# Streaming the high and the low part of the activations through a weight tile in one 512-column matmul

## The chip, the core and the metric

The program runs on one core of a Trainium2 chip. Its time is device microseconds from start to end of one execution; smaller is better. TensorE (PE in the rows) multiplies: it loads a weight tile of 128 x 128 (PEld) and streams activation columns past it. VectorE (DVE) and ScalarE (ACT) do everything elementwise, SyncE (SP) issues the transfers from HBM.

## The reference

Two transformer-like blocks over 256 tokens of width 1024. The first has four layers (short convolution, a state-space mixer, an RWKV mixer, a short convolution again), each followed by a gate and a layer norm. The second has two layers of FFN, mixer and FFN, over 256 tokens and 256 context positions. Nearly all of the arithmetic is `x @ W` with fp32 weights that are used for one set of 256 columns, or for two:

```python
def short_conv_mixer(x, w_in, conv_k, w_out):
    bg, cg, h, z = jnp.split(x @ w_in, 4, axis=-1)
    ...
    return (bg * conv * jax.nn.silu(z)) @ w_out

def first_block(...):
    for i in range(DEPTH):
        ...
        r = DN_ALPHA * x + y
        r = r + (p[i] @ ple_proj[i]) * jax.nn.sigmoid(r @ ple_gate[i])
        x = layer_norm(r, ln_g[i], ln_b[i])

def swiglu(h, w1, w3, w2):
    return (jax.nn.silu(h @ w1) * (h @ w3)) @ w2

def half_ffn(h, g, shift, scale, gate, w1, w3, w2):
    return h + 0.5 * gate[:, None, :] * swiglu(modulate(rms_norm(h, g), shift, scale), w1, w3, w2)
```

The scales, shifts and gates of the second block are products of a small condition vector with large matrices (`ada_w`).

## The kernel before

Activations lie feature-major: 128 features on the partitions, 8 chunks of features, 256 positions along the free dimension (`S = 256`, `NCH = 8`). A weight is read from HBM in blocks of 128 output columns, all 8 input chunks side by side (512 KB). `get` (lines 588 to 604) issues the transfer and splits the block into two float32r tiles whose sum it is: ScalarE copies it into `whi` (line 599), VectorE subtracts to get `wlo` (line 600). Activations are split the same way by `split` (lines 606 to 608) into the two tiles that `pair` (lines 488, 489) gives: `hi` and `lo`, each of 8 chunks x 256 columns.

`mm3` (lines 610 to 624) multiplies: for each input chunk three matmuls of 256 columns, `whi` with the high part, `whi` with the low part, `wlo` with the high part, all added up in the same 256 columns of a PSUM bank of 512. Such a group of three is called a chunk in this text, and a column tile has 8 of them (6 in the last part of an FFN). Each matmul is an instruction of its own with its own weight load, so `whi` is loaded twice. All of them are issued at line 431 (`TensorE.matmul`).

`linear` (lines 659 to 669) runs over the column tiles of a weight and gives each PSUM result to a function `take`, which differs by caller: a copy, a Tanh, a multiplication that reads PSUM directly. `finish` (lines 750 to 762) adds the mixer's result to the residual; `ffn` (lines 1396 to 1434) computes 22 pairs of tiles (`ffn_in`, in three parts of 8, 8 and 6), each pair giving one chunk of `d`, and after each part 8 tiles of `ffn_out` that are added to the residual `x` or `ctx` with a gate. `add_gated` (lines 1441 to 1445) does that for the second block's mixers. `head_tile`, `values`, `low_rank`, `key` and `ple_proj` also multiply with 256 columns. `mm3t` (lines 636 to 645) is the token-major form, where the activations are the stationary side and the weights stream; for `ab_uv` it streams 512 columns at a time.

The order of instructions is chosen when the program is built. Generators of two streams (tokens, context) are woven by `weave`, and a planner's estimate of time (`now`) decides which goes on: float32r matmuls cost columns / 2400 us and 0.002 us (lines 425, 430), VectorE and ScalarE instructions 0.07 or 0.1 us and elements / 960 or / 1200. `ada` (lines 1340 to 1359) is side work of VectorE: for each of 144 tiles two reductions over 1024 columns (`junk`, line 1354), one tile every 6.5 to 12 planner-us (`GAPS`), unless VectorE is more than `SLACK` behind in the planner's view. PSUM pool `mm`, where all the products go, has 3 banks; split weights have 4 buffers, loaded ones 4, which `ada` shares.

## Time and profile before

| what | value |
|---|---|
| median of three runs | 2930.72 us (2926.54 to 2931.11) |
| span of the profiled execution, first to last instruction | 2931.2 us |
| PE busy | 2814.3 us, 23798 matmuls |
| weight loads busy | 2652.5 us, 23798 loads |
| VectorE busy | 2142.3 us |
| ScalarE busy | 1631.4 us |
| mean granted TensorE clock | 0.985 |

The page gives no time of the profiled execution besides its span. The span is 0.1 us above the highest of the three timed runs and 0.5 us (0.02%) above their median. Matmuls overlap in the records, and their ends are modelled: the rate of TensorE is read from the distance between two starts, not from the length of one.

### The profile page before, as it was taken

What the parts mean: (1) busy time and instruction counts of PE and PEld (TensorE: products, weight loads), DVE (VectorE), ACT (ScalarE), POOL (GpSimd) and SP (SyncE); (2) the same over time, 40 slices, a digit from 0 to 9 for tenths busy, and PEclk for the clock granted to TensorE, in tenths of its full rate; (3) what the DMA queues carried; (4) which work ended last, traced back from release to release, by engine and by line L of the source; (5) the groups of instructions that cost most, each with busy time, mean ns of one, the idle gap of its engine ahead of it and who ended that gap; (6) DMA issues with size and microseconds to landing.
All of it is one profiled execution on the core that took longest, in us unless ns stands there. A gap on an engine that the chain in (4) does not pass through costs nothing.

```text
span 2931.2 us, 58792 instructions
## 1 busy us (share of the span) xinstructions
PE 2814.3 (96%) x23798; PEld 2652.5 (90%) x23798; DVE 2142.3 (73%) x4116; ACT 1631.4 (56%) x3069; POOL 16.6 (1%) x42
## 2 busy tenths in 40 slices
PE   8989998899999999999999999999999999999999
PEld 8977788787999999998999978999999999996999
DVE  8876777666678788898898887877855336676655
ACT  5644556766646464778566766544522224466443
POOL 0000000000000000000000000000000000000000
PEclk9989998999999999999999999999999999999999
DMA  7632353200466666666675644666544323221554
GB/s 266 216 130 94 100 185 123 81 23 33 140 213 203 215 201 221 205 194 190 196 224 182 194 155 129 208 223 212 181 144 125 100 82 102 92 87 57 160 182 142
DMA packets 129296, 454.89 MB, mean 155 GB/s; under 512 B 14336, under 2 KB 18688, under 8 KB 128384
## 3 DMA queue, kind: packets, MB, share of 16 engines
q1 hardware_dynamic: 129024, 451.13, 48.3%
q8 instruction: 187, 3.06, 0.4%
q14 instruction: 85, 0.70, 0.1%
HBM read 450.02 MB, written 1.05 MB: 154 GB/s over the span
## 4 chain that ended last, share of the span: by engine, by line
PE 68%; DVE 14%; DMA 8%; ACT 6%; issue 4%; SPq 0%; DVEq 0%; ACTq 0%
PE ps_mm L431 56%; DMA w<-in_ada_dram 7%; PE ps_ca L431 5%; PE ps_cb L431 5%; DVE wlo L600 5%; DVE junk L1354 3%; ACT whi L599 2%; DVE tc L402 1%; PE ps_st L431 1%; PE ps_cb L435 1%; ACT L402 1%; ACT rw_b L402 1%; ACT tc L402 1%; DVE h_lo L402 1%; DMA w<-in_ffn_in_dram 1%
## 5 line engine op out<-in xcount | busy, mean ns | idle before, releaser
L599 ACT ACTIVATE whi<-w 128x1024 fp32r<-128x1024 f32 (+1 forms) x687 | 715.9, 1044 | 731.1 <-PE ps_mm L431 474.1
L600 DVE TENSOR_TENSOR wlo<-w,whi 128x1024 fp32r<-128x1024 f32 (+1 forms) x687 | 826.3, 1204 | 240.7 <-ACT whi L599 238.8
L431 PE MATMUL ps_mm<-h_hi,whi 128*128 128x256 f32 x3024 | 868.0, 289 | 6.1 <-ACT h_hi L402 4.4
L431 PE MATMUL ps_mm<-h_lo,whi 128*128 128x256 f32 x3024 | 856.0, 284 | 2.5 <-DVE h_lo L402 2.4
L431 PE MATMUL ps_mm<-h_hi,wlo 128*128 128x256 f32 x3024 | 853.2, 283 | 3.1 <-DVE wlo L600 3.0
L431 PEld LDWEIGHTS ps_mm<-h_hi,whi 128*128 128x128 f32 x3024 | 569.7, 189 | 15.8 <-ACT h_hi L402 6.3
L431 PEld LDWEIGHTS ps_mm<-h_lo,whi 128*128 128x128 f32 x3024 | 570.2, 189 | 8.7 <-DVE h_lo L402 3.7
L431 PEld LDWEIGHTS ps_mm<-h_hi,wlo 128*128 128x128 f32 x3024 | 570.9, 189 | 7.4 <-DVE wlo L600 4.9
L1354 DVE SCALAR_TENSOR_TENSOR junk<-w,cond 128x1024 bf16<-128x1024 f32 x288 | 351.9, 1222 | 125.9 <-DMA w<-in_ada_dram 124.8
L431 PE MATMUL ps_mm<-d_hi,whi 128*128 128x256 f32 x1232 | 353.4, 287 | 0.9 <-DVE ctx L402 0.4
L431 PE MATMUL ps_mm<-d_hi,wlo 128*128 128x256 f32 x1232 | 348.5, 283 | 3.6 <-DVE wlo L600 3.6
L431 PE MATMUL ps_mm<-d_lo,whi 128*128 128x256 f32 x1232 | 349.6, 284 | 0.0
L431 PEld LDWEIGHTS ps_mm<-d_hi,wlo 128*128 128x128 f32 x1232 | 233.2, 189 | 4.9 <-DVE wlo L600 4.7
L431 PEld LDWEIGHTS ps_mm<-d_hi,whi 128*128 128x128 f32 x1232 | 232.4, 189 | 4.0 <-issue 2.6
L431 PEld LDWEIGHTS ps_mm<-d_lo,whi 128*128 128x128 f32 x1232 | 232.4, 189 | 2.7 <-issue 1.6
L402 DVE TENSOR_TENSOR td<-td,ps_mm 128x256 f32<-128x256 f32 x154 | 64.5, 419 | 82.3 <-PE ps_mm L431 78.8
L402 ACT ACTIVATE d_hi<-td 128x256 fp32r<-128x256 f32 x154 | 63.0, 409 | 79.2 <-DVE td L402 78.4
L402 ACT ACT_TABLE_LOAD x81 | 103.9, 1283 | 2.5 <-PEq L1938 0.7
L431 PE MATMUL ps_mm<-x_hi,whi 128*128 128x256 f32 x256 | 73.6, 287 | 12.4 <-ACT whi L599 12.4
L402 ACT ACTIVATE tc<-tc 128x256 f32<-128x256 f32 x182 | 75.2, 413 | 6.0 <-DVE tc L402 3.1
L402 ACT ACTIVATE td<-ps_mm 128x256 f32<-128x256 f32 x154 | 57.1, 373 | 33.5 <-PE ps_mm L431 33.1
L431 PE MATMUL ps_mm<-xs_hi,whi 128*128 128x256 f32 x256 | 72.7, 284 | 2.7 <-ACT whi L599 1.6
(459 smaller groups left out, 5466.2 us busy)
## 6 DMA issues: line engine op xcount, KB each, us to landing
w<-in_ffn_in_dram SPq DMA_DIRECT2D x268, 512.0 KB, 4.0
w<-in_ada_dram SPq DMA_DIRECT2D x144, 512.0 KB, 4.3
w<-in_ffn_out_dram SPq DMA_DIRECT2D x96, 512.0 KB, 4.1
w<-in_conv_in_dram SPq DMA_DIRECT2D x64, 512.0 KB, 4.5
w<-in_ffn_out_dram SPq DMA_DIRECT2D x48, 384.0 KB, 3.5
w<-in_ab_in_dram SPq DMA_DIRECT2D x34, 512.0 KB, 4.4
w<-in_ple_gate_dram SPq DMA_DIRECT2D x32, 512.0 KB, 4.4
w<-in_conv_out_dram SPq DMA_DIRECT2D x16, 512.0 KB, 4.6
```

Source lines behind the costliest of these rows:

```text
L402: return f(**kw)
L431: self.t.matmul(out, lhsT=lhsT, rhs=rhs, start=start, stop=stop)
L435: self.t.transpose(out, in_, ident)
L599: nc.scalar.activation(out=hi[:, :n], in_=w[:, :n], func=AF.Copy)
L600: nc.vector.tensor_tensor(out=lo[:, :n], in0=w[:, :n], in1=hi[:, :n].bitcast(F32), op=ALU.subtract)
L1354: nc.vector.scalar_tensor_tensor(out=self.junk, in0=w, scalar=1.0, in1=cb[:, s], op0=ALU.mult, op1=ALU.mult, accum_out=m[:, t, s:s + 1])
```

## The change

`pair` lays the high and the low part of a chunk side by side (two tiles of 4 chunks, each chunk 2 x 256 columns); `Part` stands for one of the parts, and `both(k)` gives the 512 columns of chunk k. `mm3w` replaces the first two matmuls of a chunk by one of 512 columns that fills the whole bank; the third goes to its first half. The two halves of the bank then have to be summed. `total` does it with a ScalarE copy of the second half to SBUF and a VectorE addition, and its result takes the place of the PSUM operand in all of `linear`'s callers but three, and in `ffn_in`. In `finish`, `add_gated` and `ffn_out` (`halves`) a second VectorE addition takes the second half from PSUM. `head_tile`, `values`, `low_rank`, `key`, `ple_proj` and `mm3t` stay as they are. The planner's price of a float32r matmul under 512 columns rises by 0.01 us, and temporaries `te` get a third buffer. The rest of the diff takes out comments.

```diff
+class Part:
+    def __init__(self, tiles, q):
+        self.tiles, self.q = tiles, q
+    def __getitem__(self, at):
+        _, k, *t = at
+        n = NCH // 2
+        if isinstance(k, slice):
+            h = k.start // n
+            return self.tiles[h][:, k.start - h * n:k.stop - h * n, self.q]
+        return self.tiles[k // n][(slice(None), k % n, self.q, *t)]
+    def both(self, k):
+        return self.tiles[k // (NCH // 2)][:, k % (NCH // 2)].rearrange("p q t -> p (q t)")
...
         if rhs.dtype == F32R:
-            dur = n / 2400.0
+            dur = n / 2400.0 + (0.01 if n < 512 else 0.0)
...
     def pair(self, i, j, name):
-        return tuple(self.slot(k, [NCH, S], f"{name}_{q}", F32R) for k, q in ((i, "hi"), (j, "lo")))
+        t = [self.slot(k, [NCH // 2, 2, S], f"{name}_{q}", F32R) for k, q in ((i, "a"), (j, "b"))]
+        return Part(t, 0), Part(t, 1)
     def tmp(self, tag, n=S):
-        b = 2 if tag in ("td", "te") else 3
+        b = 2 if tag == "td" else 3
...
+    def mm3w(self, out, w, x, m=0, k0=0, start=True, stop=True):
+        T = self.T
+        (wh, wl), (xh, _) = w, x
+        kc = wh.shape[1]
+        for k in range(kc):
+            f = lambda t: t[:, k, m * 128:(m + 1) * 128]
+            T.matmul(out, lhsT=f(wh), rhs=xh.both(k0 + k), start=start and k == 0, stop=False)
+            T.matmul(out[:, :S], lhsT=f(wl), rhs=xh[:, k0 + k], start=False, stop=stop and k == kc - 1)
+    def total(self, ps, tag="te"):
+        t = self.tmp(tag)
+        self.A.activation(out=t, in_=ps[:, S:], func=AF.Copy)
+        self.V.tensor_tensor(out=t, in0=ps[:, :S], in1=t, op=ALU.add)
+        return t
     def mm3g(self, out, w, x, m=0):
+        mm = self.mm3w if out.shape[1] > S else self.mm3
...
-            self.mm3(out, part, x, m, k, k == 0, k + PIECE >= n)
+            mm(out, part, x, m, k, k == 0, k + PIECE >= n)
...
-    def linear(self, name, x, take, kc=8, mt=1, tiles=None):
+    def linear(self, name, x, take, kc=8, mt=1, tiles=None, halves=False):
...
-                yield from self.mm3g(ps[:, :S], w, x, m)
-                take(b * mt + m, ps[:, :S])
+                wide = isinstance(x, tuple) and isinstance(x[0], Part)
+                yield from self.mm3g(ps if wide else ps[:, :S], w, x, m)
+                if halves:
+                    take(b * mt + m, ps[:, :S], ps[:, S:])
+                else:
+                    take(b * mt + m, self.total(ps) if wide else ps[:, :S])
...
-        def take(m, ps):
+        def take(m, ps, more):
             self.V.scalar_tensor_tensor(out=r[:, m], in0=x[:, m], scalar=ALPHA, in1=ps, op0=ALU.mult, op1=ALU.add)
+            self.V.tensor_tensor(out=r[:, m], in0=r[:, m], in1=more, op=ALU.add)
...
-                yield from self.mm3g(ps[:, :S], w, xs)
-                t = self.tmp("td")
-                self.act(t, ps[:, :S], AF.Silu)
+                yield from self.mm3g(ps, w, xs)
+                t = self.total(ps, "td")
+                self.act(t, t, AF.Silu)
...
-                self.V.tensor_tensor(out=t, in0=t, in1=ps[:, :S], op=ALU.mult)
+                self.V.tensor_tensor(out=t, in0=t, in1=self.total(ps), op=ALU.mult)
...
-                    T.matmul(ps[:, :S], lhsT=wh[:, k], rhs=dh[:, q], start=k == 0, stop=False)
-                    T.matmul(ps[:, :S], lhsT=wh[:, k], rhs=dl[:, q], start=False, stop=False)
+                    T.matmul(ps, lhsT=wh[:, k], rhs=dh.both(q), start=k == 0, stop=False)
                     T.matmul(ps[:, :S], lhsT=wl[:, k], rhs=dh[:, q], start=False, stop=k == n - 1)
-                self.V.scalar_tensor_tensor(out=x[:, mt], in0=ps[:, :S], scalar=gt[:, mt:mt + 1], in1=x[:, mt], op0=ALU.mult, op1=ALU.add)
+                for o in (0, S):
+                    self.V.scalar_tensor_tensor(out=x[:, mt], in0=ps[:, o:o + S], scalar=gt[:, mt:mt + 1], in1=x[:, mt], op0=ALU.mult, op1=ALU.add)
...
-        def take(k, ps):
-            self.V.scalar_tensor_tensor(out=x[:, k], in0=ps, scalar=self.m(l, i, k, s), in1=x[:, k], op0=ALU.mult, op1=ALU.add)
+        def take(k, *pss):
+            for ps in pss:
+                self.V.scalar_tensor_tensor(out=x[:, k], in0=ps, scalar=self.m(l, i, k, s), in1=x[:, k], op0=ALU.mult, op1=ALU.add)
...
-        yield from self.linear("ab_out", os_, self.add_gated(l, 5, x, s))
+        yield from self.linear("ab_out", os_, self.add_gated(l, 5, x, s), halves=True)
...
-        yield from self.linear("cd_out", outs(), self.add_gated(l, 5, x, 0))
+        yield from self.linear("cd_out", outs(), self.add_gated(l, 5, x, 0), halves=True)
```

## Rows read from the trace of the kernel before

**Rows 1.** The page: busy us by engine (share, instructions); granted clock in 40 slices.

```profile
PE 2814.3 (96%) x23798; PEld 2652.5 (90%) x23798; DVE 2142.3 (73%) x4116; ACT 1631.4 (56%) x3069; POOL 16.6 (1%) x42
...
PEclk9989998999999999999999999999999999999999
```

**Rows 2.** Timeline of PE at 2000 us: start us, length us, instruction, out<-in, shapes.

```profile
2000.04 0.28 PE L431 MATMUL ps_mm<-h_hi,whi 128*128 128x256 f32 x1
2000.15 0.28 PE L431 MATMUL ps_mm<-h_lo,whi 128*128 128x256 f32 x1
...
2002.92 0.28 PE L431 MATMUL ps_mm<-h_hi,whi 128*128 128x256 f32 x1
```

**Rows 3.** Timeline of PE at 1235 us, the 512-column products of `ab_uv`.

```profile
1235.24 0.62 PE L431 MATMUL ps_mm<-whi,kvs 128*128 128x512 f32 x2
1235.70 0.39 PE L431 MATMUL ps_mm<-wlo,kvs 128*128 128x512 f32 x1
...
1236.64 0.39 PE L431 MATMUL ps_mm<-whi,kvs 128*128 128x512 f32 x1
1236.87 0.28 PE L431 MATMUL ps_cb<-kvs,whi 128*128 128x256 f32 x1
```

**Rows 4.** Timeline of the weight loads at 2000 us.

```profile
2000.28 0.19 PEld L431 LDWEIGHTS ps_mm<-h_hi,whi 128*128 128x128 f32 x1
2000.40 0.19 PEld L431 LDWEIGHTS ps_mm<-h_lo,whi 128*128 128x128 f32 x1
```

**Rows 5.** Timeline of PE at 1745 us, float32 products of the attention.

```profile
1745.49 1.02 PE L431 MATMUL ps_ca<-kava,qa 128*128 128x512 f32 x2
1746.35 1.02 PE L431 MATMUL ps_ca<-kb,qb 128*128 128x512 f32 x2
```

**Rows 6.** Groups of matmuls by operands: xcount | busy us, mean ns | idle before, releasers.

```profile
L431 PE MATMUL ps_mm<-h_hi,whi 128*128 128x256 f32 x3024 | 868.0, 289 | 6.1 <-ACT h_hi L402 4.4 <-ACT td L402 1.0 <-DVE td L402 0.6
...
L431 PE MATMUL ps_mm<-d_hi,whi 128*128 128x256 f32 x1232 | 353.4, 287 | 0.9 <-DVE ctx L402 0.4 <-ACT d_hi L402 0.4
...
L431 PE MATMUL ps_mm<-x_hi,whi 128*128 128x256 f32 x256 | 73.6, 287 | 12.4 <-ACT whi L599 12.4
...
L431 PE MATMUL ps_mm<-mix_hi,whi 128*128 128x256 f32 x208 | 60.1, 295 | 6.3 <-ACT mix_hi L402 4.3 <-ACT whi L599 1.8 <-ACT r L402 0.2
...
L431 PE MATMUL ps_mm<-o_hi,whi 128*128 128x256 f32 x192 | 54.8, 285 | 0.0
...
L431 PE MATMUL ps_mm<-gs_hi,whi 128*128 128x256 f32 x64 | 18.0, 281 | 0.0
```

**Rows 7.** Timeline of VectorE at 1479 us.

```profile
1478.81 1.23 DVE L600 TENSOR_TENSOR wlo<-w,whi 128x1024 fp32r<-128x1024 f32 x1
1479.94 0.43 DVE L402 TENSOR_TENSOR d_lo<-td,d_hi 128x256 fp32r<-128x256 f32 x1
1480.27 1.23 DVE L1354 SCALAR_TENSOR_TENSOR junk<-w,cond 128x1024 bf16<-128x1024 f32 x1
...
1492.34 0.48 DVE L402 SCALAR_TENSOR_TENSOR x<-ps_mm,gt,x 128x256 f32<-128x256 f32 x1
1492.73 0.95 DVE L600 TENSOR_TENSOR wlo<-w,whi 128x768 fp32r<-128x768 f32 x1
```

**Rows 8.** Groups of ScalarE instructions, the same columns: reading 256 columns of PSUM.

```profile
L402 ACT ACTIVATE td<-ps_mm 128x256 f32<-128x256 f32 x154 | 57.1, 373 | 33.5 <-PE ps_mm L431 33.1
```

**Rows 9.** Stretches: length; busy us (instructions) of PE, loads, DVE, ACT, POOL; clock; DMA.

```profile
879.00:1685.00 806.00, 783.63 (x6162) 757.05 (x6161) 691.42 (x1270) 532.14 (x913) 1.45 (x6) 1.00 0.63 202
...
2125.00:2418.00 293.00, 293.00 (x2444) 293.00 (x2443) 131.81 (x206) 78.07 (x121) 0.95 (x1) 1.00 0.36 112
...
1466.00:1539.00 73.00, 72.07 (x588) 71.19 (x587) 68.67 (x120) 49.77 (x84) 0.00 (x0) 1.00 0.72 225
```

**Rows 10.** Groups of matmuls between 879 and 1685 us, columns as in Rows 6.

```profile
L431 PE MATMUL ps_mm<-h_hi,whi 128*128 128x256 f32 x1051 | 303.7, 289 | 0.8 <-DVE td L402 0.6 <-ACT h_hi L402 0.2
...
L431 PE MATMUL ps_mm<-d_hi,whi 128*128 128x256 f32 x376 | 109.3, 291 | 0.9 <-DVE ctx L402 0.4 <-ACT d_hi L402 0.4
...
L431 PE MATMUL ps_mm<-xs_hi,whi 128*128 128x256 f32 x256 | 72.7, 284 | 2.7 <-ACT whi L599 1.6 <-DVE ta L402 1.2
```

**Rows 11.** Timeline of PE at the end of the first `ple_gate`.

```profile
168.66 0.28 PE L431 MATMUL ps_mm<-rs_hi,wlo 128*128 128x256 f32 x1
172.75 0.96 PE L431 MATMUL ps_st<-total,cs_base 128*128 128x256 f32 x2 [3.81 <-DVE total L402]
```

More of the change, by code (lines that the diff above doesn't have):

```diff
@@ L754, in finish @@
         rs = None if gate in RAW else self.pair(*slots, "rs")
-        def take(m, ps):
+        def take(m, ps, more):
             self.V.scalar_tensor_tensor(out=r[:, m], in0=x[:, m], scalar=ALPHA, in1=ps, op0=ALU.mult, op1=ALU.add)
+            self.V.tensor_tensor(out=r[:, m], in0=r[:, m], in1=more, op=ALU.add)
             if rs:
                 self.split(r[:, m], rs[0][:, m], rs[1][:, m])
-        yield from self.linear(w_out, g, take)
+        yield from self.linear(w_out, g, take, halves=True)
         return r, rs
@@ L1406, in ffn @@
                 ps = self.ps()
-                yield from self.mm3g(ps[:, :S], w, xs)
-                t = self.tmp("td")
-                self.act(t, ps[:, :S], AF.Silu)
+                yield from self.mm3g(ps, w, xs)
+                t = self.total(ps, "td")
+                self.act(t, t, AF.Silu)
                 w = yield (f"ffn_in{l}{h}", 2 * m + 1, 8, 128)
                 ps = self.ps()
-                yield from self.mm3g(ps[:, :S], w, xs)
-                self.V.tensor_tensor(out=t, in0=t, in1=ps[:, :S], op=ALU.mult)
+                yield from self.mm3g(ps, w, xs)
+                self.V.tensor_tensor(out=t, in0=t, in1=self.total(ps), op=ALU.mult)
                 self.split(t, dh[:, m % 8], dl[:, m % 8])
```

## The prediction

> **What bounds the kernel now.** I read the page's busy shares first: TensorE 96% of the span, VectorE 73%, ScalarE 56%, the clock at nine tenths or more in all but two of the forty slices [rows 1]. A busy PE need not be a full one, so the next view is the timeline of PE in a dense stretch: the reader is to look at the starts, not at the lengths. From 2000.04 to 2002.92 us there are 24 steps, 0.120 us each, with no idle time between them [rows 2]. A chunk of three matmuls thus takes 0.360 us. The weight loads start as often, 0.12 us apart, each 0.19 us long and beside the matmul before [rows 4]. Then the stretches: from 2125 to 2418 us PE is busy without a gap; from 879 to 1685 us it is idle for 22.4 of 806 us while VectorE is busy for 691 (86%); and in its fullest part, 1466 to 1539 us, VectorE is busy 94% and PE still 72.07 of 73 us [rows 9]. So TensorE's stream of columns sets the time nearly everywhere, and VectorE stands close behind it in 806 us of the span.
>
> **What the change takes from TensorE.** It touches the chunks that go through the wide path. By groups [rows 6]: h has 3024 chunks, of which 320 stay as they are (40 tiles of `head_tile` and `values`: 28 of `ab_in`, 8 of `cd_k`, 4 of `cd_q`, by 8); d 1232; x, xs and rs 256 each (x stands for three equal groups); mix 208 less 16 for `low_rank`; o and g 192 each; gs and ys 64 each. The sum is 2704 + 1232 + 768 + 192 + 384 + 128 = 5408 chunks.
>
> A chunk was three matmuls of 256 columns and becomes one of 512 and one of 256. The trace of before has a 512-column float32r matmul: `ab_uv` streams its weights that way. From 1235.24 to 1236.87 us there are 7 of them [rows 3], 0.233 us each, every one with a weight load of its own, as in the new form. So a chunk costs 0.233 + 0.120 = 0.353 us: 0.007 us less, and 5408 x 0.007 = 38 us. I take this value since it is the same operation with the same number of columns and loads; only the roles of weights and activations are swapped.
>
> The bounds: the worst is that the wide matmul costs what the two did, 0.240, and the gain is 0; a loss is excluded as long as rows 3 hold, which lie below that. The best comes from the nearest row with another type: the float32 products of 512 columns start 0.43 us apart (1745.49 to 1746.35 for two) [rows 5]. I take half of that, 0.215 us, as the far end, on the assumption (no row shows it) that float32 passes over its columns twice and float32r once; it is 25 ns under the pair, and the gain is 135 us.
>
> The rows show that a load lies beside the matmul before it, and that the removed load can be worth 7 ns at most. The Trainium skill, "TensorE: Matmul & The Clock Gate", Part 2, speaks against the change here: it says that loads are pulled ahead of running matmuls and read through a port of their own, so they take nothing from the stream. By that rule the gain is 0; rows 3 against rows 2 differ from it by the 7 ns. The same page's section on the back-to-back issue gap gives N / 2.4 + 2.5 ns, which is 216 ns for 512 columns; rows 3 show 233, so the trace doesn't agree, and by that figure with 0.120 for the narrow one the gain would be about 130 us.
>
> **What it adds.** `total` runs for the tiles that aren't halved: h 338, x, xs and rs 96, mix 24, ys 8, in all 466. Each costs ScalarE a copy of 256 columns from PSUM, 0.37 us by the group of such reads [rows 8], 172 us in all; and VectorE an addition, for which I take the distance from the start of `d_lo` to the next start, 0.33 us [rows 7]: 154 us. Where the result is halved, VectorE gets a second instruction: 32 additions (g and gs) of 0.33, and 192 gated ones (168 for d, 24 for o) of 0.39, from `x` to the next start [rows 7], 85 us together. VectorE gets 239 us, ScalarE 172.
>
> Where do they lie? ScalarE has 44% idle [rows 1], so its share is hidden; without that cover it would be those 172 us. VectorE's share is hidden where PE has no use for it: from 2125 to 2418 us it is busy for 132 of 293 us [rows 9]. From 879 to 1685 us it is not safe: there are 1051 - 224 chunks of h (28 narrow tiles off), 256 of xs and 376 of d [rows 10], which is 135 tiles at 0.33 and 51 at 0.39, 65 us. VectorE then has 756 us of work in 806 - 1459 x 0.007 = 796 us, 95%. What is queued behind an addition there is the next weight's `wlo`, for which the third matmul of a chunk waits, and a PSUM bank of three is given back one addition later. Since PE lost only 0.93 of 73 us at a VectorE of 94% [rows 9], I price this at about the stretch's idle time once more, 20 us; the bounds are 0 and the whole 65.
>
> At the end of a stage there is no cover: PE waits for the last tile's chain. After the first `ple_gate` it stood from 168.66 to 172.75 us [rows 11], and the chain gets a copy and an addition longer, 0.37 + 0.33 = 0.70 us. I count ten such ends without a second stream's work or with little of it: four gates, two ends of `conv_in`, `ssm_glu`, the three parts of the last FFN. That is 7 us. The rest is small: the wide matmul needs the low part one matmul sooner (0.12 us, at the same few ends), and the new layout and the third `te` buffer cost no time. The planner's price for a chunk goes from 3 x 0.1087 = 0.326 to 0.334, while the real one falls from 0.360 to 0.353; the side work, paced by the planner, comes 4% denser. It adds about 1% to VectorE's load and is in the 20 us. No transfer changes its size or number.
>
> The sum, against the profiled execution's 2931 us, 0.02% over the median: 2931 - 38 + 20 + 7 = 2920 us.
>
> **The rivals.**
> - *The wide matmul streams at full rate.* For it: float32's 0.43 us for 512 columns [rows 5]. Against it: rows 3, the same type and width. Time: 2931 - 135 + 7, and VectorE, which then has even less time beside it, for 30: 2833 us.
> - *VectorE becomes the bound between 879 and 1685 us, and the kernel gets slower.* The added 65 us then lengthen the stretch instead of filling its idle time, and the gain is what the other 3949 chunks give, 28 us: 2931 - 28 + 65 + 7 = 2975 us. It decides as soon as VectorE can't use more than the 86% it uses now, because of waits for `whi` and for PSUM; at 95% without a hold-up it doesn't. For it: the engines take turns on every tile, with few buffers between. Against it: the 94% of 1466 to 1539 us with a full PE.
> - *The removed load was hidden altogether.* The pair and the wide one cost the same, and only the additions remain: 2931 + 0 + 20 + 7 = 2958 us. Against it: rows 3, by 7 ns of 240, which is the whole gain and not much.
>
> **How the numbers follow.** The forecast has 0.52, with a range of its own from 2890 (savings of 8 ns, no contention) to 2950 (5 ns, contention of 40); full rate 0.16, VectorE as the bound 0.20, a hidden load 0.12. A measurement can tell about 0.2%, 5.9 us, from no change. Within the forecast 0.32 lies below 2925, 0.12 within 5.9 us of the time before, 0.08 above. So faster 0.32 + 0.16 = 0.48, same 0.12, slower 0.08 + 0.20 + 0.12 = 0.40. The range goes from 2840, just above the full rate, whose upper half it takes in, to 2980, just above VectorE as the bound.
>
> **What would show it.** The distance of starts in a dense stretch: 0.353 us a chunk confirms the main term, 0.335 the first rival, 0.360 the third. Between 2125 and 2418 us PE should stay gapless and do the same work in some 6 us less. Between 879 and 1685 us the stage's length and PE's idle time tell the second rival: some 45 us idle by the forecast, 85 or more if VectorE bounds it, with `wlo` and additions as what PE waits for. The count of matmuls must fall by 5408. The forecast is wrong if the wide matmul with activations streaming is not the 0.233 us of weights streaming, or if the order of instructions that the new prices give shifts a stage by more than these terms.

## The result and the profile after

The changed kernel takes 2954.61 us (median; 2951.0 to 2955.67), the kernel before 2930.91 beside it: ratio 1.0083, interval 1.0069 to 1.0097. It is slower by 24 us, where 2920 was forecast. The profiled execution spans 2952.3 us, 0.08% under the median. All differences between kernels below are differences of such ratios times 2931 us. The interval of one ratio reaches 3 to 7 us to either side, that of a difference between two of them 4 to 9, so a few us between two kernels say nothing.

The page of the changed kernel, as in [rows 1]:

```profile
PE 2787.4 (94%) x18390; PEld 2362.1 (80%) x18390; DVE 2384.1 (81%) x4811; ACT 1790.7 (61%) x3545; POOL 16.5 (1%) x42
...
PEclk9989998999999999999999999999999999999999
```

5408 matmuls are gone, as counted. VectorE has 241.8 us more (forecast 239), ScalarE 159.3 (forecast 172). So the counts and sizes of the added work were nearly right, and still the sum was not.

The timeline of PE in a full stretch, as in [rows 2] (start us, length us, instruction, out<-in, shapes, idle time before it and what ended it):

```profile
2012.70 0.39 PE L449 MATMUL ps_mm<-d_b,whi 128*128 128x512 f32 x1
2012.93 0.28 PE L449 MATMUL ps_mm<-d_b,wlo 128*128 128x256 f32 x1
2013.05 0.39 PE L449 MATMUL ps_mm<-d_b,whi 128*128 128x512 f32 x1
...
2013.98 0.28 PE L449 MATMUL ps_mm<-d_b,wlo 128*128 128x256 f32 x1
2014.10 0.39 PE L449 MATMUL ps_mm<-d_a,whi 128*128 128x512 f32 x1
2018.35 0.39 PE L449 MATMUL ps_mm<-d_a,wlo 128*128 128x256 f32 x1 [3.86 <-DVE wlo L619]
```

From 2012.70 to 2014.10 us there are four chunks: 0.350 us each, against 0.360 in [rows 2]. The wide matmul takes 0.232, the narrow one behind it 0.118 instead of 0.120. The last line is a stall of TensorE. The timeline of VectorE shows what it did in that time:

```profile
2014.00 1.23 DVE L1396 SCALAR_TENSOR_TENSOR junk<-w,cond 128x1024 bf16<-128x1024 f32 x1 [1.30 <-DMA w<-in_ada_dram]
2015.15 0.08 DVE L1396 DVE_READ_ACCUMULATOR junk<-w,cond 128x1 f32 x1
2015.15 0.48 DVE L420 SCALAR_TENSOR_TENSOR x<-ps_mm,gt,x 128x256 f32<-128x256 f32 x1
2015.55 1.21 DVE L1396 SCALAR_TENSOR_TENSOR junk<-w,cond 128x1024 bf16<-128x1024 f32 x1
2016.69 0.08 DVE L1396 DVE_READ_ACCUMULATOR junk<-w,cond 128x1 f32 x1
2016.69 0.48 DVE L420 SCALAR_TENSOR_TENSOR x<-ps_mm,gt,x 128x256 f32<-128x256 f32 x1
2017.09 1.21 DVE L619 TENSOR_TENSOR wlo<-w,whi 128x1024 fp32r<-128x1024 f32 x1
2018.22 0.47 DVE L420 SCALAR_TENSOR_TENSOR x<-ps_mm,gt,x 128x256 f32<-128x256 f32 x1
```

In these rows VectorE does one instruction after the other. The `wlo` that PE needs stands behind a reduction that waits 1.30 us for its own transfer, a second reduction, and two gated additions, one of which is new. Nothing here is long; it stands in one line.

This stall is not the work of the sums, though. In the run without them (`e1_no_sums`, below) the same product waits longer still, 4.68 us, behind a reduction that waits 3.40 us for its transfer; with the reductions shortened (`e6_light_side` and `e7_light_no_sums`) PE does not wait there at all. It is a stall of the side work. Its line without sums:

```profile
1975.20 0.39 PE L454 MATMUL ps_mm<-d_a,wlo 128*128 128x256 f32 x1 [4.68 <-DVE wlo L625]
```

A stall that the sums do lengthen is this one, the same product in both lines. In the changed kernel it waits for `ctx`, that is, for the addition that empties a bank; without sums it waits less, and for something else:

```profile
1160.93 0.76 PE L449 MATMUL ps_mm<-d_a,whi 128*128 128x512 f32 x1 [4.60 <-DVE ctx L420]
1149.97 0.77 PE L454 MATMUL ps_mm<-d_a,whi 128*128 128x512 f32 x1 [1.83 <-ACT h_b L425]
```

The stretches of [rows 9] (length; busy us of PE, loads, VectorE, ScalarE, GpSimd; granted clock; DMA), for the second one the place where the same stage now lies, and the time after that stall:

```profile
879.00:1685.00 806.00, 765.29 (x4407) 660.23 (x4407) 733.33 (x1433) 559.34 (x1035) 1.46 (x6) 0.98 0.60 194
...
2140.00:2435.00 295.00, 295.00 (x1688) 257.34 (x1687) 196.29 (x351) 109.47 (x204) 0.95 (x1) 1.00 0.42 134
...
2019.00:2020.00 1.00, 1.00 (x6) 0.86 (x5) 1.00 (x2) 0.00 (x0) 0.00 (x0) 0.59 0.70 287
2020.00:2022.00 2.00, 2.00 (x8) 1.71 (x8) 0.22 (x1) 0.00 (x0) 0.00 (x0) 0.50 0.92 272
2022.00:2024.00 2.00, 2.00 (x12) 1.72 (x12) 1.20 (x3) 1.06 (x1) 0.00 (x0) 0.85 0.62 252
```

PE is idle for 40.7 of 806 us in the first (22.4 before), and stays gapless in the second with 844 chunks in 295 us, 0.3495 each (before: 0.360). The first stretch has the same clock times as before but not quite the same work; the section on the prediction compares the stage. The last three lines: after 3.86 us of waiting PE works at full pace for a little under 1 us, and then without a gap but at a granted clock of 0.50, the lower level of 1.2 GHz, until about 2022.5 us. Its timeline there:

```profile
2019.97 0.63 PE L449 MATMUL ps_mm<-d_b,whi 128*128 128x512 f32 x1
2020.39 0.41 PE L449 MATMUL ps_mm<-d_b,wlo 128*128 128x256 f32 x1
2020.61 0.63 PE L449 MATMUL ps_mm<-d_b,whi 128*128 128x512 f32 x1
```

A chunk takes 0.64 us instead of 0.35. So this stall cost its 4 us and then five chunks at nearly twice their time, 1.4 us more. The Trainium skill, "TensorE: Matmul & The Clock Gate", HAM oscillation section, says that waits between bursts of matmuls drop the array back to half rate, and that this is paid at every such wait; at this stall the trace agrees, with 0.50 and 0.64 us. Not every wait here has such a tail: behind one of 2.32 us that ends at 1555.84 us the granted clock stays at 1.00.

What PE waited for, in total (us, times, longest), in the changed kernel:

```profile
PE ps_mm L449 <- DVE wlo L619: 23.7, 21, 3.9
PE ps_mm L449 <- ACT whi L618: 11.6, 4, 9.5
...
PE ps_mm L449 <- DVE ctx L420: 7.8, 4, 4.6
...
PE ps_st L449 <- DVE total L420: 6.6, 2, 3.8
...
PE ps_mm L449 <- DVE te L420: 4.6, 5, 2.2
PE ps_mm L449 <- DVE td L420: 3.8, 3, 2.6
...
PE ps_mm L449 <- DVE x L420: 2.6, 2, 1.8
```

`wlo` is a weight's low part, `whi` its high part. `ctx`, `te`, `td` and `x` are written by the instructions that empty a PSUM bank: a new tile's first product waits for one of the three banks.

### The profile page after: what moved, and what is told of

It reads as the page before. It is cut to its first block, busy times and chain, and to the rows that moved or that the text cites. A ratio compares the mean times of both kernels' runs of the same rounds, so it can differ in the third digit from the quotient of the medians.

```text
span 2952.3 us, 48981 instructions
## 1 busy us (share of the span) xinstructions
PE 2787.4 (94%) x18390; PEld 2362.1 (80%) x18390; DVE 2384.1 (81%) x4811; ACT 1790.7 (61%) x3545; POOL 16.5 (1%) x42
## 4 chain that ended last, share of the span: by engine, by line
PE 72%; DVE 13%; ACT 7%; DMA 6%; issue 2%; SPq 0%; ACTq 0%; DVEq 0%
PE ps_mm L449 59%; PE ps_ca L449 6%; PE ps_cb L449 4%; DVE wlo L619 4%; DMA w<-in_ada_dram 3%; DVE junk L1396 2%; ACT whi L618 2%; DVE tc L420 1%; PE ps_st L449 1%; PE ps_cb L453 1%; ACT L420 1%; ACT rw_b L420 1%; DMA w<-in_ab_in_dram 1%; ACT tc L420 1%; DVE r L420 1%
## 5 line engine op out<-in xcount | busy, mean ns | idle before, releaser
L449 PE MATMUL ps_mm<-h_a,whi 128*128 128x512 f32 (+1 forms) x1672 | 574.1, 387 | 16.1 <-DVE h_a L420 7.3
L449 PE MATMUL ps_mm<-h_b,whi 128*128 128x512 f32 (+1 forms) x1672 | 555.0, 376 | 2.1 <-DVE h_b L420 2.1
L449 PE MATMUL ps_mm<-h_a,wlo 128*128 128x256 f32 x1512 | 431.8, 286 | 10.7 <-DVE wlo L619 10.7
L449 PE MATMUL ps_mm<-h_b,wlo 128*128 128x256 f32 x1512 | 426.3, 283 | 0.0
L449 PEld LDWEIGHTS ps_mm<-h_a,whi 128*128 128x128 f32 x1672 | 307.3, 190 | 84.7 <-issue 11.5
L449 PEld LDWEIGHTS ps_mm<-h_b,whi 128*128 128x128 f32 x1672 | 304.3, 189 | 63.4 <-DVE h_b L420 3.5
L449 PEld LDWEIGHTS ps_mm<-h_a,wlo 128*128 128x128 f32 x1512 | 287.9, 190 | 20.0 <-DVE wlo L619 15.2
L449 PEld LDWEIGHTS ps_mm<-h_b,wlo 128*128 128x128 f32 x1512 | 285.2, 189 | 2.9 <-issue 1.4
L449 PE MATMUL ps_mm<-d_a,whi 128*128 128x512 f32 x672 | 251.9, 405 | 9.6 <-DVE ctx L420 7.1
L449 PE MATMUL ps_mm<-d_b,whi 128*128 128x512 f32 x560 | 207.4, 399 | 0.9 <-DVE d_b L420 0.9
L449 PEld LDWEIGHTS ps_mm<-d_a,whi 128*128 128x128 f32 x672 | 127.9, 190 | 42.8 <-issue 8.4
```

Of the source, the lines that this page charges most:

```text
L449: self.t.matmul(out, lhsT=lhsT, rhs=rhs, start=start, stop=stop)
```

## The experiments

Three things changed at once: the matmuls, the sums, and the order of all instructions, since the planner counts with other prices. The first four runs take them apart. To hold the order, an instruction can be counted by the planner without being issued (`ghost=True`), and a matmul can be counted with another number of columns.

### Wide or narrow, with or without sums, in one order

Without the sums (`e1_no_sums`):

```diff
-        self.A.activation(out=t, in_=ps[:, S:], func=AF.Copy)
-        self.V.tensor_tensor(out=t, in0=ps[:, :S], in1=t, op=ALU.add)
+        self.A.activation(out=t, in_=ps[:, S:], func=AF.Copy, ghost=True)
+        self.V.tensor_tensor(out=t, in0=ps[:, :S], in1=t, op=ALU.add, ghost=True)
+        self.alias[t.name] = ps[:, :S]     # users of t read the bank
...
-            self.V.tensor_tensor(out=r[:, m], in0=r[:, m], in1=more, op=ALU.add)
+            self.V.tensor_tensor(out=r[:, m], in0=r[:, m], in1=more, op=ALU.add, ghost=True)
```

and likewise for the second gated additions in `ffn_out` and `add_gated`.

> The changed kernel with its wide matmuls, but the instructions that sum the halves are not issued: no copy and no addition in `total`, no second addition in `finish`, `add_gated` and `ffn_out`; the users read the first half of the bank. The planner still counts them, so the order stays that of the changed kernel. Left out of the computation: the second half (high weight by low activations) is multiplied but not added. Theory S (the sums cost the time, in VectorE's and ScalarE's queues): 5408 chunks x 9.7 ns = 52 us under the kernel before, 2879 us, 75 us less than the changed kernel. Rival O (the order that the new prices give costs the time, not the sums): within 15 us of the changed kernel's 2955, so 2940 to 2960. In between, the two share it in that proportion.

Measured: 2897.87 us, ratio 0.9889 (0.9866 to 0.9912), 56.9 us under the changed kernel. That is a quarter less than theory S's 75 and far more than rival O's 15: the sums are most of the loss, not all of it.

Narrow matmuls with the sums (`e4_narrow_sums`), and narrow ones without sums (`e5_narrow_no_sums`):

```diff
-            T.matmul(out, lhsT=f(wh), rhs=xh.both(k0 + k), start=start and k == 0, stop=False)
+            if start and k == 0:
+                T.matmul(out, lhsT=f(wh), rhs=xh.both(k0 + k), start=True, stop=False)
+            else:
+                T.matmul(out[:, :S], lhsT=f(wh), rhs=xh[:, k0 + k], start=False, stop=False, cols=512)
+                T.matmul(out[:, S:], lhsT=f(wh), rhs=xl[:, k0 + k], start=False, stop=False, cols=0)
...
# e5: both into the first half, and the sums as ghosts
+            T.matmul(out[:, :S], lhsT=f(wh), rhs=xh[:, k0 + k], start=start and k == 0, stop=False, cols=512)
+            T.matmul(out[:, :S], lhsT=f(wh), rhs=xl[:, k0 + k], start=False, stop=False, cols=0)
```

and likewise in `ffn_out`.

> The changed kernel with its sums and its order, but the first two products of a chunk are two matmuls of 256 columns again, into the two halves of the bank (the first chunk of a tile stays wide). Seven eighths of the wide matmuls' gain are given up. Theory S with TensorE still the bound: the gain was 52 us, so 2955 + 45 = 3000 us. Rival V (VectorE is the bound in the stages with much side work, so TensorE's gain was mostly lost in waiting there): much less than 45 us is given up, 2965 to 2980 us. Rival O says nothing else than S here.

Measured: 2988.03 us, ratio 1.0203 (1.0179 to 1.0226), 35 us above the changed kernel. It lies between S (45) and V (10 to 25).

> Both taken back: three matmuls of 256 columns into one half as in the kernel before, no sums, but the order of instructions, the layout of the split activations and the third `te` buffer of the changed kernel (the planner still counts wide matmuls and sums). Theory S: order and layout cost nothing, 2931 us within 6. Rival O: the order is what costs, 2945 to 2985 us.

Measured: 2947.56 us, ratio 1.0055 (1.0035 to 1.0075): 16.1 us above the kernel before. Rival O holds here for its part: the same matmuls, the same elementwise work, another order, and 16 us. The layout of the split activations and the third `te` buffer came with it; no run separates them from the order. One difference can be counted: 692 splits of weights where the kernel before has 687. What that costs no run shows.

The three runs and the two kernels make a table of differences to the kernel before (us):

| | no sums | sums |
|---|---|---|
| narrow, order of before | 0 | |
| narrow, order of after | +16.1 | +59.5 (an eighth of it wide) |
| wide, order of after | -32.5 | +24.3 |

So the wide matmuls give 48.7 us where nothing else is added, 9.0 ns a chunk; the sums cost 56.9 us beside wide matmuls and some 49 beside narrow ones (43, and 6 for the eighth that is wide), where PE needs longer for a tile; and the order costs 16.1. 16.1 - 48.7 + 56.9 = 24.3 us, the whole result, since these are the steps from one kernel to the next; each is sure to 6 to 9 us.

That the order matters shows elsewhere too. The changed kernel with the planner's old price (`e2_old_price`):

```diff
-            dur = n / 2400.0 + (0.01 if n < 512 else 0.0)
+            dur = n / 2400.0
```

> The changed kernel with the planner's old price of a narrow float32r matmul (columns / 2400, without the added 0.01 us). The planner then believes a chunk to cost 0.324 us instead of 0.334. Theory S: nothing but noise of the order, 2955 us within 8. Rival O, in the form that the new price is at fault: 2935 us or less.

Measured: 2937.66 us, ratio 1.0026 (1.0016 to 1.0036), 16.7 us under the changed kernel. Theory S missed (within 8 us of 2955); rival O (2935 or less) missed by 3 us and is the nearer. This order is neither that of before nor that of the changed kernel, so it proves no figure for the latter. The new price by itself, in the kernel before (`e3_before_new_price`, the same line the other way round):

> The kernel before, with one edit: the planner's price of a float32r matmul under 512 columns is 0.01 us higher, as in the changed kernel. Nothing else changes but the order that the planner finds. If the new price makes the order worse by itself: 2940 us or more. If the 17 us of order that the changed kernel carries come with the price only beside the counted sums: 2931 us within 6.

Measured: 2969.51 us, ratio 1.0133 (1.0117 to 1.0150): 39 us slower from 0.01 us in a planner's table. And with the side work's pace stretched in proportion (`e17_price_pace`, `GAPS = (7.1, 10.9, 13.1, 13.1)`):

> The kernel before with the new price (2969 us), and the side work's intervals longer by 9% (`GAPS` 7.1, 10.9, 13.1, 13.1), as the planner's time for three matmuls is. If the 39 us came from side work that the higher price makes denser in real time: back to 2931 us within 10. If from the order in which the streams' instructions are woven: 2950 us or more.

Measured: 2977.25 us, ratio 1.0165 (1.0148 to 1.0182). The denser side work is not the reason; how the streams' instructions are woven is what is left. Four orders of the same narrow work lie 0 (`e11_same_order_narrow`, below), 16, 39 and 48 us above the kernel before, and I found no rule in them.

### What in the sums costs

The side work on VectorE shortened (`junk` over 64 columns instead of 1024), with and without sums:

```diff
-  nc.vector.scalar_tensor_tensor(out=self.junk, in0=w, scalar=1.0, in1=cb[:, s], ...)
+  nc.vector.scalar_tensor_tensor(out=self.junk[:, :64], in0=w[:, :64], scalar=1.0, in1=cb[:, s, :64], ...)
```

> The changed kernel, with the two reductions of each `ada` tile over 64 columns instead of 1024 (the transfer stays whole, the planner's price too). Left out of the computation: all but the first 64 columns of those products, so the modulation is another. VectorE loses about 288 x 1.0 us of work. To be compared with the next run, which is the same without the sums. Theory C (the additions cost by standing in VectorE's queue among the side work): the sums cost less than 20 us here instead of 57, so less than 20 us over the next run. Rival H (they cost by what they add to the chain of a tile, the copy, the addition and the later PSUM bank, whatever else VectorE does): 45 us or more over the next run.

> The same shortened reductions in the changed kernel without its sums (left out: the second half of each bank, and all but 64 columns of the `ada` products). Gives the base for the run before. By itself: between 2870 and 2898 us; the side work cost at most the 28 us of waits for `wlo` and for norms that are left without the sums.

Measured: ratios 0.9905 (0.9885 to 0.9924) and 0.9751 (0.9735 to 0.9767), 2899.75 and 2855.31 us. Without sums the side work had cost 40 us, more than I had set as the most. The sums cost 45 us here instead of 57. So side work in VectorE's queue makes the sums dearer by about 12 us, with an error of some 11; theory C, my own from the prediction, is at most a part of the matter. Rival H (45 or more) is just met.

Only the copies (`e8_copies_only`: the copy issued, the addition a ghost), and only the second additions of the halved results (`e13_halves_only`: the copies and additions of `total` as ghosts):

> The changed kernel with the copies of `total` on ScalarE (466 of 0.37 us) but without any of the 690 instructions that they add to VectorE; the users read the first half. Left out of the computation: the second half is not added. Order of the changed kernel. Theory C: near the run without copies and additions, 2898 to 2910 us. Rival A (ScalarE's queue is at fault: the copies delay `whi`): 2935 us or more.

> The changed kernel in its order, without the copies and additions of `total` (466 tiles), but with the second additions of `finish`, `add_gated` and `ffn_out` (224 instructions of VectorE, some 81 of its 239 us of added work). Left out of the computation: the second half of the banks that `total` sums. Theory Q: in proportion to VectorE's time, 2898 + 19 = 2917 us. Theory W: these additions wait for no other engine than before, 2898 to 2908 us.

Measured: ratios 0.9971 (0.9958 to 0.9984) and 0.9977 (0.9967 to 0.9987), 24 and 26 us above the run without sums. Both theories missed on the copies: 466 copies that nobody reads, on an engine that was idle 44% of the time, cost 24 us. In the prediction they cost nothing. They did not do it by delaying weights, as rival A has it: PE waits 16.0 us for `whi` and 9.7 for `wlo`, against 14.1 and 10.9 in the run without sums; what grew are waits for other results of ScalarE, `pp` from 0.5 to 6.0 and `td` from 2.4 to 5.5. On the additions theory W missed, and Q (19) came nearer: 224 instructions on VectorE cost some 0.12 us each, though each only follows one that had to wait anyway.

The same amount of work, on data that nothing waits for (`e10_loose_sums`):

```diff
+        nc.scalar.activation(out=t, in_=src, func=AF.Copy)                       # src: a constant
+        nc.vector.tensor_tensor(out=self.junk[:, :S], in0=src, in1=src, op=ALU.add)
```

> The changed kernel without its sums, as in the run without copies and additions (2898 us), but with the same number of copies (ScalarE) and additions (VectorE) of 128 x 256 elements on a constant tile: the same work, for which nothing waits and which waits for nothing, so it may slip to other places of its engine's queue. Left out of the computation: the second half of each bank. Theory Q (the time that the sums take of VectorE and ScalarE is what costs): near the changed kernel, 2940 to 2955 us. Theory W (their place costs: they wait for the tile's last matmul and for each other, with weight splits and other tiles' work behind them in the queues, and the tile's result comes later): 2898 to 2912 us.

Measured: 2906.62 us, ratio 0.9921 (0.9906 to 0.9935). Its page:

```profile
PE 2766.3 (95%) x18390; PEld 2350.0 (81%) x18390; DVE 2376.0 (82%) x4810; ACT 1788.3 (62%) x3550; POOL 16.5 (1%) x42
```

VectorE and ScalarE are as busy as in the changed kernel (2384.1 and 1790.7 us), with as many instructions, and the kernel is 47 us faster. The work as such costs 9 us, with an error of 8; the other 47 come from where it stands. This is theory W (2898 to 2912), and against theory Q: equal busy shares go with a difference of 47 us. Two limits of the run: the loose instructions read SBUF where the sums read PSUM, and not all of the copies are free of waits. Before the 154 into `td` ScalarE is idle for 89 us in all, until their buffer is free:

```profile
L667 ACT ACTIVATE td<-cs_base 128x256 f32<-128x256 f32 x154 | 63.6, 414 | 89.2 <-DVE d_a L425 50.9 <-DVE d_b L425 37.9
```

Two groups of the changed kernel (busy us, mean ns, then idle time of the engine just before them and what ended it) show the standing:

```profile
L420 ACT ACTIVATE te<-ps_mm 128x256 f32<-128x256 f32 x314 | 115.6, 370 | 51.5 <-PE ps_mm L449 51.0
```

```profile
L420 DVE TENSOR_TENSOR te<-ps_mm,te 128x256 f32<-128x256 f32 x312 | 129.8, 417 | 39.1 <-ACT te L420 37.9
```

ScalarE stands for 51 us at the head of its queue until PE has ended a tile, and VectorE for 38 us until ScalarE has copied it; what is queued behind waits too, and a late PE makes them both late. How much of the 57 us comes of that these rows don't tell: a wait at the head of ScalarE's queue is not dear by itself, as the 89 us of the loose copies show.

### Is it the weights behind, or the banks?

What can stand behind a sum is a weight's split; what stands before PE is a bank. First, the second additions put behind the next tile's weight split (`e14_delayed`):

```diff
+  late = m1 < 22 or last
+  if late and mt:
+      self.tc.keep_in_program_order(second())    # the tile before's second half
   for o in (0, S):
-      self.V.scalar_tensor_tensor(out=x[:, mt], in0=ps[:, o:o + S], ...)
+      self.V.scalar_tensor_tensor(out=x[:, mt], in0=ps[:, o:o + S], ..., ghost=late and o > 0)
+  second = lambda mt=mt, ps=ps: nc.vector.scalar_tensor_tensor(out=x[:, mt], in0=ps[:, S:], ...)
+  if late and mt == NCH - 1:
+      second()
```

The last tile of each of the 15 parts keeps its second addition in place, so 105 of the 120 move.

> The changed kernel, with one edit: in `ffn_out` (all parts after which no squares are taken, 120 of the 168 tiles) the second addition of a tile is issued after the next tile's weight split instead of right behind the first addition. Same work, same planner's order. Theory W1 (the sums cost because weight splits stand behind them in VectorE's queue): the second additions cost 25 us in all, 224 of them; for the 120 that move, up to 13 us come back: 2941 to 2950 us. Rival W2 (they cost because their own tile's bank and result are ready later): no gain or a loss, since these results come later still: 2953 us or more.

Measured: 2960.92 us, ratio 1.0109 (1.0093 to 1.0125), 7.6 us above the changed kernel. W2 holds; W1's gain did not come. The run also keeps the banks longer, so the time alone would not refute W1. PE's waits say more:

```profile
PE ps_mm L449 <- DVE wlo L619: 23.9, 23, 3.6
PE ps_mm L449 <- ACT whi L618: 11.5, 3, 9.7
PE ps_mm L449 <- DVE te L420: 9.1, 12, 2.2
```

Those for weight parts are as long as in the changed kernel (23.7 and 11.6), so taking the additions out of the way of the splits did not bring the splits sooner where PE waits for them; those for `te` doubled. Then four banks in one ring instead of three and one, with and without sums:

```diff
-        self.psum = {n: self.pool(es, "p_" + n, b, PSUM) for n, b in BANKS.items()}
+        self.psum = {n: self.pool(es, "p_" + n, b, PSUM) for n, b in dict(mm=4, ca=2, cb=2).items()}
+        self.psum["st"] = self.psum["mm"]
```

> The changed kernel, with the PSUM bank of the pool `st` (sums over partitions) put into the pool `mm`: four banks that products and those sums use in turn, instead of three and one. The planner still counts three and one, so the order stays. Theory B (a tile's sum gives its bank back later, and the first matmul of a coming tile waits for it): the sums' cost, which is this run less the next, falls from 57 us to 40 or less. Rival W1 (weight splits come late behind the sums): it stays above 50.

> The same four banks in the changed kernel without its sums (2898 us with three and one). Left out of the computation: the second half of each bank. By theory B banks are hardly waited for here, so 2885 to 2900 us; the products that end a norm (`st`) now wait in the same ring, which may cost some us.

Measured: ratios 1.0053 (1.0038 to 1.0068) and 0.9872 (0.9854 to 0.9889), 2943.48 and 2893.29 us. The fourth bank helps the changed kernel by 9 us; the 5 us of the one without sums are within the errors. The sums still cost 53 us, within the errors the 57 of before. Theory B (40 or less) falls as the one cause; that the cost stays above 50 is what rival W1 had forecast here. The waits of the changed kernel with four banks tell why:

```profile
PE ps_mm L449 <- DVE wlo L620: 27.8, 28, 4.0
PE ps_mm L449 <- ACT whi L619: 17.0, 7, 9.5
...
PE ps_mm L449 <- DVE te L420: 1.3, 3, 0.6
```

The waits for `te` fell from 4.6 to 1.3 us, and those for `ctx`, `td` and `x` are no longer among the thirty longest, but `wlo` rose from 23.7 to 27.8 and `whi` from 11.6 to 17.0. The stall had changed its name: with three banks the sums show at the banks, with four at the weights.

In the run without sums and with three banks the waits for weights, and the one for `total`, read:

```profile
PE ps_mm L454 <- ACT whi L624: 14.1, 4, 10.5
PE ps_mm L454 <- DVE wlo L625: 10.9, 11, 4.7
...
PE ps_st L454 <- DVE total L425: 3.6, 2, 2.8
```

Last, where does the 57 us stand in TensorE's time? I took every distance between two starts on PE in the run without sums and in the changed kernel, and put what exceeds the full-clock distance (0.232, 0.118 to 0.120 us) under what ended the idle time, or, where PE was not idle and the distance was about twice that, under the low clock:

| us over full pace | no sums | sums | more |
|---|---|---|---|
| idle until a result of VectorE or ScalarE is there, or a bank | 21.5 | 42.8 | 21.3 |
| idle until a weight part is there | 18.0 | 30.0 | 12.0 |
| idle before sums over partitions, attention and the like | 18.7 | 24.2 | 5.5 |
| not idle, at half the clock | 36.9 | 50.1 | 13.2 |
| not idle, other short delays | 30.3 | 34.7 | 4.4 |
| sum | 125.4 | 181.8 | 56.4 |

Nearly a quarter of what the sums cost is not waiting at all, but slow chunks, as after 2019 us above. Counted in the same way, the run with loose sums has some 27 us of idle time for weight parts, 22 for results or banks, and 35 at half the clock. So work in VectorE's and ScalarE's queues that no product needs already makes the splits of weights late, and this is about its 9 us; the longer waits for results and banks and the slow chunks come only with the sums in their place.

### A version that beats both

Set stage against stage, the run without sums and the changed kernel drift apart by 2 us up to the weights of the second `conv_in` (885 and 887 us), by 32 more until the second `ab_out` (1785 and 1819), by 20 more until `cd_f` (2391 and 2445), and by 4 after that. So the wide form was kept where the sums cost little: `conv_in0`, `conv_out0` and the FFNs (1,0) and (1,1), with the old price (`e9_wide_slack`):

```diff
+WIDE = ('conv_in0', 'conv_out0', 'ffn10', 'ffn11')
...
+                wide = isinstance(x, tuple) and isinstance(x[0], Part) and name in WIDE
```

> Wide matmuls and sums only where the comparison of the runs with and without sums shows small cost: `conv_in0`, `conv_out0`, and the FFNs (1,0) and (1,1); three narrow matmuls without sums elsewhere, with the planner's old price. Gain 9.2 ns x about 1850 chunks = 17 us, cost of the sums there about 3 us: 2931 - 14 = 2917 us if the order does no harm. Rival: by the order the time moves 10 us either way, 2907 to 2927; rival H: sums cost everywhere alike, 690 tiles for 57 us, here about 270 of them for 22 us: 2936 us.

Measured: 2913.35 us, ratio 0.9954 (0.9937 to 0.9971). And the same order with narrow matmuls everywhere and no sums (`e11_same_order_narrow`):

> The kernel with wide matmuls in four stages only (2913 us), in its order, with three narrow matmuls into one half and no sums everywhere. Its difference to that kernel is the net worth of the wide form in those stages. If the wide form earns what was worked out (17 us of matmuls less 3 of sums), 2927 us; if that kernel's lead over the kernel before is only a better order, 2918 us or less.

Measured: 2930.00 us, ratio 1.0000 (0.9989 to 1.0012). The 13.5 us (with an error of 6) are the wide form's own, not a luckier order's: 1904 chunks at 9.0 ns are 17 us, and the sums there cost 4.

Then the `ffn_out` stages of all other FFNs too, where a tile takes only one more instruction of VectorE and none of ScalarE, the planner's order untouched; without and with the delay of the second addition (the diff of the delay is the one above):

```diff
-                    if wide:
-                        T.matmul(ps, lhsT=wh[:, k], rhs=dh.both(q), start=k == 0, stop=False)
-                    else:
-                        T.matmul(ps[:, :S], lhsT=wh[:, k], rhs=dh[:, q], start=k == 0, stop=False)
-                        T.matmul(ps[:, :S], lhsT=wh[:, k], rhs=dl[:, q], start=False, stop=False)
+                    T.matmul(ps, lhsT=wh[:, k], rhs=dh.both(q), start=k == 0, stop=False, cols=None if wide else 516.8)
```

> The same without the delay: each second addition right behind the first. By the price of 25 us for 224 (0.11 us each): 2913 - 6.5 + 11 = 2918 us. If these stages have slack: 2907 us.

> The kernel with wide matmuls in four stages (2913 us), with its order, plus wide matmuls in the `ffn_out` stages of the other FFNs (704 chunks, 96 tiles with one more addition), the second addition issued after the next weight's split where no squares follow. The planner isn't told. Gain 704 x 9.2 ns = 6.5 us; cost, by the 25 us for 224 such additions, 11 us if they stood in front, less behind the split. W1: 2908 to 2914 us; W2: 2917 us or more.

Measured: 2904.51 us, ratio 0.9912 (0.9896 to 0.9928), and 2914.50 us, ratio 0.9952 (0.9938 to 0.9967). The first is the best of all complete versions, 26 us under the kernel before. Its page:

```profile
PE 2781.6 (96%) x21190; PEld 2501.1 (86%) x21190; DVE 2266.2 (78%) x4457; ACT 1687.6 (58%) x3235; POOL 16.5 (1%) x42
```

The delayed run lies between W1 (2914 at most) and W2 (2917 or more), but the delay costs 11.7 us, a second time against W1. The 12 us from the 704 chunks have an error of 7, so the 6.3 that 9.0 ns each give are within it.

## Why the prediction was wrong, step by step

- *The chunk's price.* The mechanism was right, the size low: 0.353 us forecast from [rows 2] and [rows 3], 0.350 measured; 38 us forecast, 48.7 measured by the two runs without sums. The gap is 2 to 3 ns a chunk, most of it the narrow matmul behind a wide one (0.118, not 0.120), and 5408 chunks make 11 us of it. The Trainium skill, "TensorE: Matmul & The Clock Gate", Part 2, says that loading the next weights takes no read bandwidth from the running matmul. By that a removed load would be worth 0, as the rival of the hidden load has it; a removed pair of load and matmul is worth 9 ns here, which part of the pair is open. The full-rate rival would have needed 0.215 us for 512 columns, and 0.232 was measured; that float32 passes over its columns twice, which its price assumed, no run shows.
- *The counts.* 5408 matmuls, 690 instructions on VectorE with 242 us, 159 us on ScalarE: right.
- *The copies at nothing.* This step failed. ScalarE's 44% of idle time was named as the cover for 172 us of copies. Alone they cost 24 us. Idle time of an engine is cover only for work that can move into it; a copy that waits for the last matmul of a tile can't, and what ScalarE does for PE after it comes later.
- *VectorE at 20 us plus stage ends at 7.* This step failed too, in size and in place. The sums cost 57 us, not 27. I had read VectorE's share from 879 to 1685 us and, with 45%, from 2125 to 2418 us [rows 9], and took everything after 1685 us to be like the second. The stretch between, in the kernel before:

```profile
1789.00:2064.00 275.00, 272.80 (x2236) 267.60 (x2234) 207.34 (x329) 144.49 (x221) 0.00 (x0) 1.00 0.64 203
```

  VectorE is 75% busy there, and in the changed kernel 84% with 18.5 us of PE's time idle, of which about half is there without sums too (9.7 us, last line):

```profile
1819.00:2100.00 281.00, 262.51 (x1437) 220.26 (x1436) 236.20 (x422) 156.53 (x265) 0.00 (x0) 0.98 0.59 188
```

```profile
1785.00:2052.00 267.00, 257.33 (x1441) 218.59 (x1438) 202.96 (x328) 138.00 (x211) 0.00 (x0) 0.99 0.62 201
```

  In the stretch that was priced the waiting came out well, but not the cost: 40.7 us of idle PE between 879 and 1685 us, 45 forecast. The stage from the second `conv_in` to the second `ab_out` shows it, in the kernel before, without sums and with them:

```profile
882.00:1789.00 907.00, 883.12 (x6805) 832.03 (x6803) 775.86 (x1461) 596.26 (x1034) 1.45 (x6) 1.00 0.61 195
```

```profile
885.00:1785.00 900.00, 875.86 (x5079) 743.22 (x5079) 774.80 (x1454) 607.40 (x1045) 1.45 (x6) 0.99 0.61 197
```

```profile
887.00:1819.00 932.00, 889.32 (x5090) 751.81 (x5088) 850.19 (x1692) 655.30 (x1209) 1.46 (x6) 0.98 0.59 190
```

  The sums make it 32 us longer. Idle PE is 18.5 us of that, close to the 20 forecast; the other 13.5 are busy time, at a lower granted clock, which no idle time shows. And the argument from [rows 9] that PE lost little beside a VectorE of 94% said nothing on added work, since that work's place differs: the loose copies and additions raise VectorE's share just as much and cost 9 us.
- *Stage ends.* Seven us for ten ends is not refuted as far as the rows go: PE's idle time before sums over partitions, attention and the like is 5.5 us longer with sums (the table above). No run isolates the ends. The first `ple_gate`'s end, 4.09 us in [rows 11], on PE's timeline after the change:

```profile
162.97 0.28 PE L449 MATMUL ps_mm<-rs_b,wlo 128*128 128x256 f32 x1
166.06 1.22 PE L449 MATMUL ps_st<-total,cs_base 128*128 128x256 f32 x2 [2.80 <-DVE total L420]
```

  It is 3.09 us, shorter in spite of the longer chain; and in the run without sums, in the same order, PE waits 2.84 us there, as long as the 2.80 with them. The 0.70 us for a longer chain don't show at this end. Why, no run tells.
- *The order.* This step failed too: counted at nothing, with one sentence on what would make the forecast wrong. It cost 16 us (with layout and buffers), a third of the gain. The kernel that was measured was not the change alone, but the change and a new schedule.
- *The rivals.* "The load is hidden altogether" has nearly the right time, 2958 us, for a wrong reason: the chunk did get cheaper. "VectorE is the bound" was the nearest in kind, but not by its condition: at 91% in that stretch VectorE was not full, and emptying its queue of side work returned some 12 us of 57.

What stays open: the 57 us don't split into causes that add up. Copies alone cost 24, second additions alone 26, the work without its waits 9; less side work takes 12 off (error 11), a fourth bank 4 (error 10). Taking one wait away brought the next one forward, so I can say which waits are there (the table above) but not a price for each. Late splits of weights are 12 of the 57 us in the table, and 9 of these come with the loose work too. Delaying the second additions behind the splits gained nothing, and the copies alone leave the waits for weights as they were; with four banks, though, the waits for weights are the ones that grew. More buffers for split weights were not tried.

## What to carry to other kernels

Price added elementwise work by where it waits, not by the idle share of its engine: here 242 + 159 us of it cost 9 us where no product waited for it and 57 us between a tile's last matmul and its bank's return. A wait of TensorE can have a tail at half the clock (13 of the 57 us here), so look at the chunks behind a stall before pricing it. And where a planner chooses the order, compare within one order (count the work, don't issue it) before believing a difference of 1%: a price changed by 0.01 us moved the unchanged kernel by 39 us.

## What the runs showed of the hardware that I had not expected

- A 512-column float32r matmul is 0.232 us with activations streaming, against 0.233 with weights streaming in [rows 3]; a 256-column one behind it takes 0.118 us, behind another 256-column one 0.120.
- After a wait of 3.86 us TensorE fell to the lower of its two clock levels (granted clock 0.50 from 2020 to 2022 us) although it had been busy again for nearly 1 us: 0.64 us a chunk instead of 0.35. In the whole changed kernel such chunks take 50 us more than at the full clock, in the kernel before 35, by the count above.
- 690 instructions on VectorE and 466 on ScalarE, on constants and mostly without waits, slow this kernel, which TensorE bounds, by 0.3% (9 us, with an error of 8), with VectorE 82% and ScalarE 62% busy.
